# Moving 32 tokens of layer 0 from the dense expert product to the row gather

## The chip, the cores and the metric

The kernel runs on one core of a Trainium2 chip. The metric is the device time of one execution in microseconds (us). TensorE is called PE here, its weight loads PEld, VectorE is DVE, ScalarE is ACT, GpSimd is POOL, and SyncE (SP) only issues DMAs.

## What is computed

Two layers of a diffusion backbone run over 256 latent and 256 context tokens of width 1024. Each layer has a token mixer and then a PEER block, and the change is in the PEER block of layer 0, which all 512 tokens pass. PEER holds 16384 experts per layer; an expert is one row `u` and one row `v` of 1024 numbers. Each token has 8 heads, each head picks 16 experts, so a token uses 128 of them:

```
act = gelu(einsum('td,thkd->thk', xb, u_tab[eid]), approximate=False)
return einsum('thk,thkd->td', gate * act, v_tab[eid])
```

`eid` (which experts) and `gate` (a softmax over the 16 of a head) come from a routing step ahead of this.

## The kernel before

The PEER block is computed in two ways side by side.

**Dense.** Three of the four 128-token tiles of layer 0 (tiles 0, 1 and 3, so 384 tokens) are multiplied with all 16384 experts, 128 experts at a time; an "expert block" e is one of these 128 groups. `First.mm` makes the products with `u` (24 matmuls of 384 columns per block, in three split terms that keep fp32 accuracy), `First.gelu` applies the Gelu, `weigh` multiplies with the gate matrix `G` (zero for experts that a token did not pick) and splits the product `w` into `ww`, and `mm_v` multiplies with `v` (18 matmuls of 512 columns: three tiles, three split terms, two halves) into the PSUM tiles `y`. The gate matrix is built ahead of the loop, one block of 16 tokens at a time, from 0/1 rows (`find`, `weigh`, `join`, `keep`), stored in DRAM as `gd`, and read back every eighth iteration (`load_G`).

**Gathered.** Tile 2 (128 context tokens, one per partition) is computed by `gather_uv`: 128 indirect DMAs from POOL fetch one `u` row per token (`row`), DVE multiplies each with the tokens `h2` and sums it into `coef`; after a Gelu and the gate, 128 more DMAs fetch `v` rows and DVE adds them, weighted, into `f`. Six row buffers are used in turn (`NROW`).

**The order.** The main loop of `dense_experts` runs e from 0 to 127, and `in_order` holds every engine to the order in which its instructions are written. Layer 0 has worked 27 blocks of the `u` product ahead (`AHEAD0`), so iterations 0 to 100 hold a `u` product and a `v` product, and iterations 101 to 127 only the `v` product. In one iteration ACT does `act` (Gelu), `vh` (cast of a `v` block), `ww` (cast of `w`), `uh` (cast of a `u` block); DVE does `w`, `vl`, the low part of `ww`, and then the adds of the rows that the iteration before fetched; POOL does `ul` (the low part of a `u` block) and then fetches new rows. SP loads `ur` and `vr`, one block of each per iteration, in a queue of its own. How many rows have been fetched by the end of iteration e is the list `quota`: GRATE rows per iteration, and at least so many that GTAIL per iteration are left for the end. Both kinds of `row` operation stand in the helper at L859, L865 and L871; casts and low parts stand at L154 and L155.

Layer 1 works in the same way with 192 dense tokens and 64 gathered ones, which lie twice on the partitions with four heads each.

Of the kernel before, what the change touches and what calls it, by code (L numbers as in the profile page):

```python
# [19 lines left out]
D = 1024  # L20
T = 256
# [16 lines left out]
GRATE, GTAIL, HRATE = 2.4, 0.7, 1.1  # L38
# [4 lines left out]
def backbone(ctx: ExitStack, tc: tile.TileContext, x, cx, ccT, ada_w, ada_b, ada_rows, n1g, n2g, ev_in, ev_out,  # L43
# [806 lines left out]
    def gather_uv(f, eid, gate, h2, pool, quota):  # L850


        S = eid.shape[1]
        coef = pool.tile([128, S], F32, tag="coef", name="coef", bufs=1)
        r = {}

        def fetch(n):
            r[n] = pool.tile([128, D], F32, tag="row", name="row", bufs=NROW)
            nc.gpsimd.indirect_dma_start(out=r[n], out_offset=None, in_=v_tab if n >= S else u_tab,  # L859
                                         in_offset=bass.IndirectOffsetOnAxis(ap=eid[:, n % S:n % S + 1], axis=0))  # L860

        def add(n):
            t, j = r.pop(n), n - S
            if n < S:
                nc.vector.scalar_tensor_tensor(t, t, 1.0, h2, op0=OP.mult, op1=OP.mult, accum_out=coef[:, n:n + 1])  # L865
# [8 lines left out]
        for n in [*quota, 2 * S]:  # L874
# [59 lines left out]
    def dense_experts(l, slots, hi, lo, tiles, g2, upools, first, rows, half=False):  # L934
# [4 lines left out]
        ntok = nt * 128 - 64 * half  # L939
# [5 lines left out]
        with ExitStack() as st:  # L945
# [79 lines left out]
            def mm_v(*es):  # L1025
                ops = [ws.pop(e) + vs.pop(e) for e in es]
                for j in (range(nt - 1, -1, -1) if half and 127 in es else range(nt)):
                    c = slice(j * 128, (j + 1) * 128)
                    for e, (ww, vh, vl) in zip(es, ops):
                        if half and j == nt - 1:  # L1030
                            both = ww[:, full:full + 128]
                            sums = (both, vh), (both, vl)
                        else:
                            low = ww[:, 2 * ntok - full + j * 128:][:, 0:128]
                            sums = (ww[:, c], vh), (ww[:, c], vl), (low, vh)
                        for n, (x1, x2) in enumerate(sums):
                            for d in range(2):
                                nc.tensor.matmul(y[j][:, d, :], x1, x2[:, d * 512:(d + 1) * 512],  # L1038
# [3 lines left out]
            f = rp.tile([128, D], F32, tag="f", name="f")  # L1042
            if half:
                quota = [min(128, int(HRATE * (e + 1))) for e in range(128)]
# [3 lines left out]
            ys = [] if half else [(rows[0], f)]  # L1048
# [25 lines left out]
            for _ in side:  # L1074
                pass
            ab_stack.close()
# [3 lines left out]
            with in_order():  # L1080
                if half:
                    tk, yy = ys.pop()
                    t, z = (vb.tile([128, D], F32, tag="t4", name=n) for n in ("yl", "yz"))
                    nc.sync.dma_start(z[64:128], f[0:64])
# [186 lines left out]
```

## Time and profile before

| | us |
|---|---|
| median of 3 runs (lowest, highest) | 2750.55 (2741.23, 2753.81) |
| the profiled execution, whole | 2754.86 |
| its span, first to last instruction | 2752.8 |
| PE busy in the span | 2570.1 (93%) |
| DVE busy | 2055.0 (75%) |
| ACT busy | 1120.4 (41%) |
| POOL busy | 1043.0 (38%) |
| share of PE in the chain of waits that ended last | 70% |

The busy share is an average over stages that have different limits. What a change in one stage is worth is read from that stage: which wait ends last there. Four stretches of layer 0 matter here: the building of the gate matrix (from about 556 to 692 us), the main loop with `u` and `v` products (712 to 1571 us), the end of that loop with `v` products alone (1571 to 1697 us), and the routing ahead of all this.

### The profile page before, as it was taken

The page shows a single profiled execution, that of the slowest core. Times are in us where ns is not written, and L with a number is a line of the kernel's source. Part 1 is how long each engine was busy: PE and PEld are TensorE (multiplying, and loading weights), DVE is VectorE, ACT ScalarE, POOL GpSimd, SP SyncE. Part 2 cuts the span into 40 slices and gives each one's busy share as a digit, 9 for nine tenths or more (in the row PEclk, how much of TensorE's full clock was granted, in tenths as well). Part 3 has the DMA queues.
Part 4 walks back from the last instruction along what each step waited for, and adds up shares of the span by engine and source line. Part 5 has one row for each costly group of instructions (what it writes and reads, how often), then busy time and mean ns, then how long its engine had stood idle before and what let it go on. Part 6 is the DMA issues. An engine that isn't in the chain of part 4 may idle for free.

```text
span 2752.8 us, 39475 instructions
## 1 busy us (share of the span) xinstructions
PE 2570.1 (93%) x14787; PEld 2237.7 (81%) x14787; DVE 2055.0 (75%) x3753; ACT 1120.4 (41%) x1832; POOL 1043.0 (38%) x643
## 2 busy tenths in 40 slices
PE   7899996899999999999999998989859999999997
PEld 4776775899989888899898876756859899999995
DVE  3535579898677776677677776787888788888888
ACT  3234432444333333333333334234535455555543
POOL 0201042300477677667766610100520344434431
PEclk9999997899999999999999998999979999999999
DMA  8562431255888888888888875632537999999996
GB/s 285 178 207 96 138 99 33 85 207 221 293 288 287 288 287 297 286 294 298 296 308 279 289 251 165 226 129 89 179 108 257 341 347 345 348 349 332 355 326 217
DMA packets 263552, 667.80 MB, mean 243 GB/s; under 512 B 21760, under 2 KB 108544, under 8 KB 258752
## 3 DMA queue, kind: packets, MB, share of 16 engines
q1 hardware_dynamic: 204176, 458.81, 48.9%
q0 software_dynamic: 55296, 201.35, 20.2%
q10 hardware_dynamic: 3888, 5.11, 0.6%
q8 instruction: 116, 1.90, 0.3%
q14 instruction: 76, 0.62, 0.1%
HBM read 621.88 MB, written 42.47 MB: 241 GB/s over the span
## 4 chain that ended last, share of the span: by engine, by line
PE 70%; DVE 13%; issue 5%; POOL 5%; DMA 4%; ACT 1%; ACTq 0%; POOLq 0%; SPq 0%; DVEq 0%
PE y L1038 24%; PE u_ps L911 9%; PE u_ps L910 9%; PE u_ps L909 9%; PE g_ps L985 4%; PE z_ps L318 2%; PE z_ps L319 2%; PE z_ps L320 2%; POOL ul L155 2%; POOL row L859 2%; DMA w<-in_ada_w_dram 1%; PE trp L170 1%; PE q_ps L806 1%; PE q_ps L807 1%; PE q_ps L805 1%
## 5 line engine op out<-in xcount | busy, mean ns | idle before, releaser
L909 PE MATMUL u_ps<-hi,uh 128*128 128x384 f32 (+1 forms) x2048 | 635.7, 310 | 42.8 <-ACT uh L154 35.6
L1038 PE MATMUL y<-vh,ww 128*128 128x512 f32 x2304 | 661.4, 397 | 7.0 <-ACT ww L1019 6.1
L911 PE MATMUL u_ps<-hi,ul 128*128 128x384 f32 (+1 forms) x2048 | 637.5, 311 | 24.8 <-POOL ul L155 13.9
L910 PE MATMUL u_ps<-lo,uh 128*128 128x384 f32 (+1 forms) x2048 | 634.6, 310 | 0.0
L1038 PEld LDWEIGHTS y<-vh,ww 128*128 128x128 f32 x2304 | 425.0, 189 | 95.0 <-ACT ww L1019 11.4
L859 POOL DMA_INDIRECT row<-in_u_tab_dram,eid x192 | 291.4, 1518 | 424.4 <-DVE w L1015 152.0
L909 PEld LDWEIGHTS u_ps<-hi,uh 128*128 128x128 f32 x2048 | 396.0, 193 | 53.7 <-ACT uh L154 36.9
L911 PEld LDWEIGHTS u_ps<-hi,ul 128*128 128x128 f32 x2048 | 395.2, 193 | 32.5 <-POOL ul L155 20.4
L154 ACT CAST vh<-vr 128x1024 fp32r<-128x1024 f32 x256 | 267.7, 1046 | 368.4 <-PE y L1038 339.1
L1038 PE MATMUL y<-vl,ww 128*128 128x512 f32 x1280 | 402.7, 395 | 0.1
L910 PEld LDWEIGHTS u_ps<-lo,uh 128*128 128x128 f32 x2048 | 395.6, 193 | 8.7
L155 POOL TENSOR_TENSOR ul<-ur,uh 128x1024 fp32r<-128x1024 f32 x116 | 311.0, 2682 | 240.0 <-ACT uh L154 238.7
L865 DVE SCALAR_TENSOR_TENSOR row<-row,h 128x1024 f32<-128x1024 f32 x192 | 299.7, 1577 | 112.6 <-DMA row<-in_u_tab_dram,eid 112.3
L859 POOL DMA_INDIRECT row<-in_v_tab_dram,eid x192 | 288.9, 1505 | 245.0 <-DVE w L1015 142.0
L155 DVE TENSOR_TENSOR vl<-vr,vh 128x1024 fp32r<-128x1024 f32 x256 | 312.4, 1220 | 73.3 <-ACT vh L154 73.0
L871 DVE SCALAR_TENSOR_TENSOR f<-row,coef,f 128x1024 f32<-128x1024 f32 x190 | 289.9, 1526 | 100.2 <-DMA row<-in_v_tab_dram,eid 98.7
L1038 PEld LDWEIGHTS y<-vl,ww 128*128 128x128 f32 x1280 | 240.4, 188 | 59.3 <-DVE vl L155 3.9
L154 ACT CAST uh<-ur 128x1024 fp32r<-128x1024 f32 x256 | 268.3, 1048 | 20.3 <-DMA ur<-in_u_t_dram 10.9
L1019 ACT CAST ww<-w 128x384 fp32r<-128x384 f32 (+1 forms) x256 | 110.7, 432 | 330.5 <-DVE w L1015 211.6
L155 DVE TENSOR_TENSOR ul<-ur,uh 128x1024 fp32r<-128x1024 f32 x140 | 171.4, 1224 | 83.9 <-ACT uh L154 83.7
L916 ACT ACTIVATE act<-u_ps 128x384 f32<-128x384 f32 (+1 forms) x256 | 105.1, 410 | 284.8 <-PE u_ps L911 284.7
L151 POOL TENSOR_TENSOR rs<-rs,nhalf 128x4 f32<-128x4 f32 (+2 forms) x19 | 22.4, 1177 | 461.4 <-DVE rs L150 347.6
(270 smaller groups left out, 3755.9 us busy)
## 6 DMA issues: line engine op xcount, KB each, us to landing
ur<-in_u_t_dram SPq DMA_DIRECT2D x256, 512.0 KB, 5.6
vr<-in_v_tab_dram SPq DMA_DIRECT2D x256, 512.0 KB, 6.1
w<-in_ada_w_dram SPq DMA_DIRECT2D x96, 512.0 KB, 4.7
gd<-stage SPq DMA_DIRECT2D x36, 1024.0 KB, 4.8
G<-gd SPq DMA_DIRECT2D x16, 1536.0 KB, 11.9
w<-in_w_q_dram SPq DMA_DIRECT2D x64, 256.0 KB, 3.4
w<-in_od_in_dram SPq DMA_DIRECT2D x24, 512.0 KB, 5.4
G<-gd SPq DMA_DIRECT2D x16, 768.0 KB, 8.6
```

What stands on the lines that cost most here:

```text
L154: nc.scalar.copy(hi, src)
L155: (eng or nc.vector).tensor_tensor(lo, src, hi.bitcast(F32), op=OP.subtract)
L859: nc.gpsimd.indirect_dma_start(out=r[n], out_offset=None, in_=v_tab if n >= S else u_tab, in_offset=bass.IndirectOffsetOnAxis(ap=eid[:, n ...
L865: nc.vector.scalar_tensor_tensor(t, t, 1.0, h2, op0=OP.mult, op1=OP.mult, accum_out=coef[:, n:n + 1])
L871: nc.vector.scalar_tensor_tensor(f, t, coef[:, j:j + 1], f, op0=OP.mult, op1=OP.add)
L909: nc.tensor.matmul(p, uh[:, k, :], hi[:, k, 0:n], start=k == 0, stop=False)
L910: nc.tensor.matmul(p, uh[:, k, :], lo[:, k, 0:n], start=False, stop=False)
L911: nc.tensor.matmul(p, ul[:, k, :], hi[:, k, 0:n], start=False, stop=k == KD - 1)
L916: nc.scalar.activation(a, self.ps.pop(e), AF.Gelu)
L985: nc.tensor.matmul(v["p"][t // 4][:, t % 4, :], o2[:, t // 4, :, t % 4], o1[:, t // 4, :, t % 4], start=n == 0, stop=n == 1)
L1019: nc.scalar.copy(ww[:, 0:ntok], w)
L1038: nc.tensor.matmul(y[j][:, d, :], x1, x2[:, d * 512:(d + 1) * 512], start=e == 0 and n == 0, stop=e == 127 and n == len(sums) - 1)
```

## The change

32 of the 384 dense tokens of layer 0, the last 32 of tile 3, are taken out of the dense product and are gathered too. They lie four times on the 128 partitions, each quarter with two of the eight heads, so 32 more `u` rows and 32 more `v` rows are fetched per partition (`eid4`, `gate4`, `h4`). Their sums `f1` (one per quarter) are joined by a product with `quarters`, a 128 x 32 matrix of zeros and ones, straight into the last 32 partitions of `y[2]`.

- The `u` product has 352 columns in place of 384, and `act`, `w` and `ww` shrink alike. The `v` product keeps its 18 matmuls of 512 columns per block; for tile 3 they have 96 rows of output. The gate matrix has 22 blocks in place of 24.
- `gather_uv` works through two sets one after the other: 256 and then 64 rows. GRATE goes from 2.4 to 2.75 and GTAIL from 0.7 to 1.3.
- `turn_back` transposes twice as much per call and makes one more copy; three DMAs copy `h4` to the other quarters. `done` gets two DVE operations and four small DMAs per half of the heads.

```
-GRATE, GTAIL, HRATE = 2.4, 0.7, 1.1
+GRATE, GTAIL, HRATE = 2.75, 1.3, 1.1
...
-    def gather_uv(f, eid, gate, h2, pool, quota):
+    def gather_uv(sets, pool, quota):
+        todo = []
+        for f, eid, gate, h2 in sets:
+            S = eid.shape[1]
+            coef = pool.tile([128, S], F32, tag=f"coef{S}", name="coef", bufs=1)
+            todo += [(m, S, f, eid, gate, h2, coef) for m in range(2 * S)]
...
-                            low = ww[:, 2 * ntok - full + j * 128:][:, 0:128]
+                            low = ww[:, (2 * ntok - full + j * 128 if c.stop <= full else ntok):][:, 0:n_j]
...
-                quota = [min(256, int(GRATE * (e + 1)), 256 - int(GTAIL * max(0, 124 - e))) for e in range(128)]
-            side = gather_uv(f, *rows[1:], rp, quota)
+                quota = [min(total, int(GRATE * (e + 1)), total - int(GTAIL * max(0, 124 - e))) for e in range(128)]
+            side = gather_uv([(f, *r[1:]) for f, r in zip(fs, rows)], rp, quota)
...
+            if full < ntok and not half:
+                for d in range(2):
+                    nc.tensor.matmul(y[nt - 1][96:128, d, :], quarters, fs[-1][:, d * 512:(d + 1) * 512], start=True, stop=True,
+                                     tile_position=(0, 96))
...
-                    nc.scalar.copy(h2[:, k2 * 256:(k2 + 1) * 256].rearrange("p (k d) -> p k d", k=2),
-                                   transposed([h[:, k, 128:256] for k in range(2)]))
+                    p = transposed([h[:, k, c:c + 128] for c in (128, 0) for k in range(2)])
+                    c = slice(k2 * 256, k2 * 256 + 256)
+                    nc.scalar.copy(h2[:, c].rearrange("p (k d) -> p k d", k=2), p[:, 0:2])
+                    nc.scalar.copy(h4[96:128, c].rearrange("p (k d) -> p k d", k=2), p[96:128, 2:4])
+                    if k2 == 3:
+                        for g in range(3):
+                            nc.sync.dma_start(h4[32 * g:32 * g + 32], h4[96:128])
...
+                    b, eidi = slice(96, 128), wk([128, 64], "eidi", I32)
+                    nc.vector.scalar_tensor_tensor(eidf, i12[:, 0, 1, c], 128.0, i12[:, 1, 1, c], op0=OP.mult, op1=OP.add)
+                    nc.vector.tensor_copy(eidi, eidf)
+                    for g in range(2):
+                        to, h = slice(32 * (2 * r + g), 32 * (2 * r + g) + 32), slice(32 * g, 32 * g + 32)
+                        nc.sync.dma_start(eid4[to], eidi[b, h])
+                        nc.sync.dma_start(gate4[to], gate[b, 1, r * 64 + 32 * g:r * 64 + 32 * g + 32])
...
-                first = First(0, hi, lo, 384, upools)
+                first = First(0, hi, lo, 352, upools)
...
-        dense_experts(0, sl, hi, lo, (0, 1, 3), mod[5], upools, first, (2, eid, R[1][1][:, 0, :], h2))
+        dense_experts(0, sl, hi, lo, (0, 1, 3), mod[5], upools, first, 352,
+                      [(2, eid, R[1][1][:, 0, :], h2), (None, eid4, gate4, h4)])
```

The places where the change moves instructions: POOL at the start of the main loop, where `ul` is the low part of a `u` block and `row` a fetch. Before:

```order
L859 DMA row<-in_u_tab_dram,eid 128x1024 x2
L155 TENSOR_TENSOR ul<-ur,uh 128x1024
L859 DMA row<-in_u_tab_dram,eid 128x1024 x3
L155 TENSOR_TENSOR ul<-ur,uh 128x1024
L859 DMA row<-in_u_tab_dram,eid 128x1024 x2
L155 TENSOR_TENSOR ul<-ur,uh 128x1024
L859 DMA row<-in_u_tab_dram,eid 128x1024 x3
```

POOL at the same place now:

```order
L863 DMA row<-in_u_tab_dram,eid 128x1024 x3
L155 TENSOR_TENSOR ul<-ur,uh 128x1024
L863 DMA row<-in_u_tab_dram,eid 128x1024 x3
L155 TENSOR_TENSOR ul<-ur,uh 128x1024
L863 DMA row<-in_u_tab_dram,eid 128x1024 x3
L155 TENSOR_TENSOR ul<-ur,uh 128x1024
L863 DMA row<-in_u_tab_dram,eid 128x1024 x2
```

Three of four iterations fetch three rows now, where two of five did; the iteration with two rows is every fourth.

POOL around the last `ul`, after which the `v` products run alone. Before:

```order
L155 TENSOR_TENSOR ul<-ur,uh 128x1024
L859 DMA row<-in_v_tab_dram,eid 128x1024 x2
L155 TENSOR_TENSOR ul<-ur,uh 128x1024
L859 DMA row<-in_v_tab_dram,eid 128x1024 x17
L151 TENSOR_TENSOR rs<-rs,nhalf 128x2 x2
```

POOL at the same place now (`eid_2798` is `eid4`):

```order
L155 TENSOR_TENSOR ul<-ur,uh 128x1024
L863 DMA row<-in_u_tab_dram,eid_2798 128x1024 x3
L155 TENSOR_TENSOR ul<-ur,uh 128x1024
L863 DMA row<-in_u_tab_dram,eid_2798 128x1024 x13
L863 DMA row<-in_v_tab_dram,eid_2798 128x1024 x32
```

Behind the last `ul` stood 17 fetches; now 45 stand there.

SP's queue at the end of routing now, where `gate_2799` is `gate4`; before, the 11 loads of `ur` stood without a break:

```order
L901 DMA ur<-in_u_t_dram 128x1024 x10
L1164 DMA eid_2798<-eidi 32x32
L1165 DMA gate_2799<-gate_2971 32x32
L1164 DMA eid_2798<-eidi 32x32
L1165 DMA gate_2799<-gate_2971 32x32
L901 DMA ur<-in_u_t_dram 128x1024
L996 DMA gd_4830<-stage 128x2048
```

The eleventh load of `ur` now stands behind four copies that wait for the routing's last results.

## Rows read from the trace of the kernel before

**Rows 1.** Windows: us, busy us of each engine (instructions), PE clock, DMA share, GB/s

```profile
401.00:556.00 155.00, 115.97 (x567) 103.48 (x566) 146.40 (x638) 52.01 (x84) 45.24 (x36) 0.85 0.18 57
556.00:692.00 136.00, 132.19 (x979) 128.35 (x979) 116.07 (x99) 65.78 (x111) 1.24 (x2) 0.94 0.58 217
692.00:712.00 20.00, 17.88 (x92) 17.23 (x91) 6.20 (x7) 6.37 (x10) 0.87 (x1) 0.91 1.04 355
712.00:1571.00 859.00, 850.95 (x4227) 766.64 (x4226) 620.28 (x671) 297.23 (x404) 601.42 (x341) 1.00 0.84 291
1571.00:1697.00 126.00, 121.13 (x507) 96.53 (x506) 83.29 (x107) 41.66 (x57) 15.40 (x14) 0.97 0.73 243
```

**Rows 2.** Chain that ended last: start, us, what; main loop and its end

```profile
716.88 4.18 PE y L1038 x18
725.29 4.18 PE y L1038 x18
733.69 4.18 PE y L1038 x18
...
1571.50 14.89 PE y L1038 x65
```

**Rows 3.** Groups by line, 712 to 1571 us: busy, mean ns, idle before and releaser

```profile
L911 PE MATMUL u_ps<-hi,ul 128*128 128x384 f32 x809 | 275.7, 341 | 8.0 <-POOL ul L155 7.7
L155 POOL TENSOR_TENSOR ul<-ur,uh 128x1024 fp32r<-128x1024 f32 x100 | 271.9, 2719 | 218.6 <-ACT uh L154 218.2
L865 DVE SCALAR_TENSOR_TENSOR row<-row,h 128x1024 f32<-128x1024 f32 x128 | 222.1, 1756 | 112.6 <-DMA row<-in_u_tab_dram,eid 112.3
L1019 ACT CAST ww<-w 128x384 fp32r<-128x384 f32 x101 | 51.8, 513 | 170.0 <-DVE w L1015 166.2 <-PE u_ps L911 3.6
```

**Rows 4.** Timeline, one round of ACT, POOL, DVE with three rows [idle before]

```profile
848.96 0.51 ACT L1019 CAST ww<-w 128x384 fp32r<-128x384 f32 x1 [0.52 <-DVE w L1015]
...
850.51 2.41 POOL L155 TENSOR_TENSOR ul<-ur,uh 128x1024 fp32r<-128x1024 f32 x1 [0.84 <-ACT uh L154]
...
853.07 1.76 POOL L859 DMA_INDIRECT row<-in_u_tab_dram,eid  x1
855.13 1.67 POOL L859 DMA_INDIRECT row<-in_u_tab_dram,eid  x1 [0.30 <-issue]
857.11 1.80 POOL L859 DMA_INDIRECT row<-in_u_tab_dram,eid  x1 [0.30 <-issue]
...
864.94 1.23 DVE L865 SCALAR_TENSOR_TENSOR row<-row,h 128x1024 f32<-128x1024 f32 x1 [1.35 <-DMA row<-in_u_tab_dram,eid]
...
866.76 0.52 ACT L1019 CAST ww<-w 128x384 fp32r<-128x384 f32 x1 [1.51 <-DVE w L1015]
```

**Rows 5.** Timeline of ACT: casts that close the first and last three-row rounds

```profile
781.84 0.51 ACT L1019 CAST ww<-w 128x384 fp32r<-128x384 f32 x1 [1.30 <-DVE w L1015]
...
1552.45 0.51 ACT L1019 CAST ww<-w 128x384 fp32r<-128x384 f32 x1 [1.37 <-DVE w L1015]
```

**Rows 6.** The same for rounds with two rows, first and last

```profile
807.48 0.51 ACT L1019 CAST ww<-w 128x384 fp32r<-128x384 f32 x1 [1.73 <-DVE w L1015]
...
1560.77 0.51 ACT L1019 CAST ww<-w 128x384 fp32r<-128x384 f32 x1 [1.28 <-DVE w L1015]
```

**Rows 7.** Groups by line, 1571 to 1697 us

```profile
L155 DVE TENSOR_TENSOR vl<-vr,vh 128x1024 fp32r<-128x1024 f32 x26 | 31.8, 1224 | 42.1 <-ACT vh L154 42.1
L871 DVE SCALAR_TENSOR_TENSOR f<-row,coef,f 128x1024 f32<-128x1024 f32 x17 | 21.7, 1278 | 1.4 <-DMA row<-in_v_tab_dram,eid 1.4
L1022 DVE TENSOR_TENSOR ww<-w,ww 128x384 fp32r<-128x384 f32 x26 | 14.3, 551 | 0.0
```

**Rows 8.** Timeline near 1671 us: ACT's wait for a `v` block, then PE

```profile
1671.61 1.04 ACT L154 CAST vh<-vr 128x1024 fp32r<-128x1024 f32 x1 [10.23 <-DMA vr<-in_v_tab_dram]
...
1673.12 1.22 PE L1038 MATMUL y<-vh,ww 128*128 128x512 f32 x2 [4.40 <-ACT ww L1019]
...
1679.12 0.62 PE L1038 MATMUL y<-vl,ww 128*128 128x512 f32 x2
```

**Rows 9.** Chain that ended last, gate matrix: start, us, what

```profile
565.99 7.57 PE g_ps L985 x64
577.79 3.79 PE g_ps L985 x32
```

**Rows 10.** Groups by line, whole span: fp32 products of one 32-partition group

```profile
L211 PE MATMUL mod_ps<-w,silu_c 128*32 128x256 f32 x512 | 45.7, 425 | 14.7 <-DMA w<-in_ada_w_dram 8.9 <-ACT silu_c L95 5.8
```

**Rows 11.** Timeline of ACT, norm ahead of routing: one copy of `turn_back`

```profile
337.69 0.37 ACT L1126 COPY h<-trp 128x256 f32<-128x256 f32 x1 [1.28 <-PE trp L170]
```

More of the change, by code (lines that the diff above doesn't have):

```diff
@@ L873, in gather_uv @@
         done = 0
-        for n in [*quota, 2 * S]:
+        for n in [*quota, len(todo)]:
             for m in range(len(r) + done, n):
@@ L932, in step, with dense_experts @@
                 next(self.steps, None)
-    def dense_experts(l, slots, hi, lo, tiles, g2, upools, first, rows, half=False):
+    def dense_experts(l, slots, hi, lo, tiles, g2, upools, first, ntok, rows):
         nt = len(slots)
-        ntok = nt * 128 - 64 * half
+        half = ntok % 128 == 64
         ntc = ntok // 16
@@ L1037, in mm_v @@
                             for d in range(2):
-                                nc.tensor.matmul(y[j][:, d, :], x1, x2[:, d * 512:(d + 1) * 512],
+                                nc.tensor.matmul(y[j][0:n_j, d, :], x1, x2[:, d * 512:(d + 1) * 512],
                                                  start=e == 0 and n == 0, stop=e == 127 and n == len(sums) - 1)
             rp = st.enter_context(pool_(name="rp", bufs=1))
-            f = rp.tile([128, D], F32, tag="f", name="f")
+            fs = [rp.tile([128, D], F32, tag=f"f{n}", name=f"f{n}") for n in range(len(rows))]
+            total = sum(2 * r[1].shape[1] for r in rows)
             if half:
-                quota = [min(128, int(HRATE * (e + 1))) for e in range(128)]
+                quota = [min(total, int(HRATE * (e + 1))) for e in range(128)]
             else:
-                quota = [min(256, int(GRATE * (e + 1)), 256 - int(GTAIL * max(0, 124 - e))) for e in range(128)]
-            side = gather_uv(f, *rows[1:], rp, quota)
-            ys = [] if half else [(rows[0], f)]
+                quota = [min(total, int(GRATE * (e + 1)), total - int(GTAIL * max(0, 124 - e))) for e in range(128)]
+            side = gather_uv([(f, *r[1:]) for f, r in zip(fs, rows)], rp, quota)
+            ys = [(r[0], f) for f, r in zip(fs, rows) if r[0] is not None]
             for e in range(VAHEAD[l]):
@@ L1114, in expert_pools @@
             yield hi, lo, route_pools
+    quarters = const.tile([128, 32], F32, name="quarters")
+    nc.vector.tensor_add(quarters, ident[:, 0:32], ident[:, 32:64])
+    for g in (2, 3):
+        nc.vector.tensor_add(quarters, quarters, ident[:, g * 32:g * 32 + 32])
     with expert_pools(0, 512, 384, AHEAD0) as (hi, lo, route_pools):
@@ L1119, in backbone @@
         eid = gp.tile([128, 128], I32, tag="eid", name="eid")
-        h2 = gp.tile([128, D], F32, tag="h2", name="h2")
+        eid4 = gp.tile([128, 32], I32, tag="eid4", name="eid4")
+        gate4 = gp.tile([128, 32], F32, tag="gate4", name="gate4")
+        h2, h4 = (gp.tile([128, D], F32, tag=n, name=n) for n in ("h2", "h4"))
         with banks(4, 2):
@@ L1183, in backbone @@
                         slots_T(sl[i], [i12[:, 0, i, :], i12[:, 1, i, :], gate[:, i, :]])
-        dense_experts(1, sl, hi, lo, (0, 1), mod1[5], upools, first, (1, eid, hgate, h2), True)
+        dense_experts(1, sl, hi, lo, (0, 1), mod1[5], upools, first, T - 64, [(None, eid, hgate, h2)])
     fin = P["small"] = ctx.enter_context(pool_(name="fin", bufs=2))
```

23 lines of the change are left out of this document (12 added, 11 removed).

## The prediction

> **What bounds the kernel now.** I read the windows by stage first. In the main loop (712 to 1571 us) PE is busy 851 of 859 us at full clock, while DVE, ACT and POOL are busy 620, 297 and 601 us; while the gate matrix is built PE is busy 132 of 136 us; at the end, with `v` products alone, 121 of 126 us; in the routing it is DVE, 146 of 155 us [rows 1]. So from 556 us on the short answer is PE. The chain of waits says the same: the `v` products start every 8.40 to 8.41 us, and one takes 4.18 us, so a `u` product takes the other 4.22 us [rows 2].
>
> But 100 periods, from the first start to the one at 1571.50, take 854.6 us, or 8.55 each: 0.14 us more than PE's own 8.41 [rows 2]. So something reaches PE now and then, and the groups by line say what. PE waited for POOL's `ul`, though only 7.7 us in all. POOL waited 218 us for the cast `uh`, ACT waited 166 us for DVE's `w`, and DVE waited 112 us for rows that POOL had fetched [rows 3]. These waits form a ring, and one round of it is in the timeline: cast `ww` at 848.96, then `uh` on ACT, `ul` on POOL at 850.51, three fetches at 853.07, 855.13 and 857.11, the third row landed and added at 864.94 (7.8 us after its issue), `w`, and `ww` again at 866.76 [rows 4]. That is 17.80 us, and it spans two iterations, for which PE needs 16.82 us. The ring is slower than PE in this round; PE notices little, because `ww` and `ul` are ready some us ahead of their use.
>
> I measured all 98 rounds in this stretch, each from a `ww` to the second `ww` behind it, by the number of rows fetched in between. The 39 with three rows average 17.73 us, the 59 with two 16.71 us; 34 and 43 of them end in a wait for DVE, and of those the closing casts of the first and the last are shown [rows 5, 6]. The mix, 0.4 x 17.73 + 0.6 x 16.71 = 17.12, or 8.56 a period, is the 8.55 of the chain. **PE and the ring are level now**: that is the point on which the forecast rests.
>
> **The main loop.** The change shortens each `u` matmul by 32 of 384 columns: 4.22 x 32/384 = 0.35 us per block, so that PE's own period becomes 8.06 us. It also puts three rows where two stood: the pattern 2, 2, 3, 2, 3 becomes 2, 3, 3, 3. The third row costs the ring one more POOL issue (2.06 us from start to start in [rows 4]) and one more landing. With the measured rounds, 0.75 x 17.73 + 0.25 x 16.71 = 17.48, or 8.74 a period. `w`, `ww` and its low part shrink by a twelfth (some 0.05 us each of 0.5), so I take 8.72. Over 100 periods: 872 - 854.6 = **+17 us**. The bounds: if PE kept the pace with today's loss of 0.14, 8.20 a period, -35 us; if the strand of rounds that never has a two-row iteration set the pace (the two-row iteration is every fourth, so it always falls into the same one of the two interleaved rings), 17.73 / 2 = 8.87, +32 us. The value taken lies near the upper one because the two kinds of round are measured, and a PE pace of 16.12 us for two periods is below the mean of both.
>
> On the 0.35 us: the trace gives 4.22 / 24 = 0.176 us from one `u` matmul to the next. The Trainium skill (TensorE: Matmul & The Clock Gate, section "Wait — 56ns, not 53.3ns?") has N / 2.4 GHz and a fixed 2.5 ns, which would be 0.163 us; by it the fixed part doesn't shrink, and the saving would be 0.32 us per block. PE's period would then be 8.09, and the lower bound 3 us less of a gain.
>
> **The end, `v` products alone.** 28 blocks of 4.18 us are 117 us; the stretch takes 126. The difference is a wait of 4.40 us for `ww` that waited for a `v` block, and what followed: the matmuls from 1673.12 to 1679.12 ran at about half rate (1.22 us for a pair against 0.62), some 2.7 us [rows 8]. The order of POOL's queue shows 45 fetches behind the last `ul` now, where 17 stood. These 28 rows have to be moved, and added at 1.28 us each [rows 7]. If spread evenly they would fit: DMA moves 243 GB/s there, and in the stretches at 0.84 and 1.04 of its share 291 and 355 GB/s, so about 345 is full; 126 us leave room for 12.9 MB, or 24 rows of 0.524 MB, and DVE has 43 us idle for 36 us of adds [rows 1, 7]. They aren't spread: up to about iteration 108 the rate stays at 2.75 rows. An iteration then moves 3.75 x 0.524 MB = 1.97 MB, 5.7 us at 345 GB/s, and DVE needs 0.5 + 1.22 + 0.5 + 2.75 x 1.28 = 5.7 us too; PE needs 4.18. Eight iterations cost 12 us. The two loads of G that fall into this stretch, 1.4 MB each, meet fuller queues than now; I add one more wait such as the one shown, with its slow matmuls, 7 us. **+19 us**; at least 0 (spread and hidden), at most 28 x 1.52 = +43 us (every row on the path).
>
> **The gate matrix.** Two blocks of 24 go, each 3.79 us of PE (7.57 for two) [rows 9], and 12 `u` products in this stretch save 0.35 us each: 7.6 + 4.2 = **-12 us**. PE is the limit there; DVE, next at 116 us, loses work with the same two blocks. The other 15 products ahead of the loop lie beside the routing, where DVE is the limit, or beside the loads at 692 to 712 us with DMA at 1.04 [rows 1], and save nothing.
>
> **What is added ahead of the loop and behind it.** Four more ACT copies of at most 0.37 us [rows 11] stand in the norm; four more DVE operations of 64 columns in the routing cost less than the 0.55 us of one of 384 columns each [rows 7]. The DMAs of `h4` stand on SP ahead of later `w_q` loads, those of `eid4` and `gate4` ahead of the eleventh `ur` load, which has three buffers and is needed only blocks later: nothing, if that cover holds, and a few us of the routing if not. The join is two fp32 products on 32 output partitions with 512 columns; the nearest row has 0.425 us for 256 columns [rows 10], so at most 1.7 us, and DVE still has a tile to gate then. Together **+3 us**, from 0 to +6.
>
> **Sum.** +17 + 19 - 12 + 3 = +27 us on the profiled execution of 2754.9 us: 2782. That execution lies 4.3 us above the median of the three runs, so the forecast of the median is **2778 us**.
>
> **The rivals.**
> - *PE keeps the pace in the main loop (faster).* For it: in calm stretches `ww` isn't late at all, and PE's waits sum to only 8 us [rows 3]. If POOL and DVE hinder each other only where both read at once, an iteration needs `ul` 2.41 [rows 4], and DVE's 0.5 + 1.22 + 0.5 and 1.22 per row: 8.29 with three rows, 7.07 with two, mean 7.98, under 8.06. This is the lock of the Trainium skill (SBUF — State Buffer, section "Who interferes with whom"): VectorE operations with two SBUF inputs and GpSimd operations that read SBUF exclude each other. The trace agrees that they do: the add takes 1756 ns on average beside `ul`, 1278 without [rows 3, 7]. Against it: the latency of the rows isn't in that sum, and the rounds show it. Price: -35 + 12 - 12 + 3 = -32, so 2719 us.
> - *The ring stays at today's 8.55 (no change).* Rounds with two rows were partly held at PE's pace, and could be shorter without it; a load of G that disturbs the ring is a little smaller. Main loop 0, the end +9, then -12 and +3: 2751 us.
> - *The end runs out of DMA (slower still).* Six fetched rows, a `v` block and G queue together, `v` blocks come late again and again, and PE, idle often, falls to the lower clock as at 1673 us. Together with the slower strand in the main loop: +32 + 43 - 12 + 3 = +66, so 2817 us. It decides from the point where two blocks of `v` ahead no longer cover the queue.
> - That the change doesn't do what it says is excluded by the order: 22 gate blocks, 352 columns, 45 fetches at the end.
>
> **How the numbers follow.** The forecast has 0.45, with a range of its own of 2762 to 2795 (8.65 to 8.80 a period, the end +10 to +27); PE's pace 0.22, no change 0.20, the end 0.13. A measurement of this kernel can tell about 0.5% from no change, here 13.8 us. From 2719 to 2817 leaves about half of the fastest and half of the slowest case out, less than 2 in 10. Faster: the first rival and a little of the second, 0.23. Within: most of the second and the lower end of the forecast, 0.20. Slower: 0.57.
>
> **What would show it.** In the profile after: starts of `v` products about 8.7 us apart in the main loop with PE waiting for `ul` and `ww` for many us (the rival: 8.1 and hardly any); rounds of two iterations still near 17.7 us; PE busy well under 99% there; the stretch with `v` products alone about 145 us, its first eight iterations at 5 to 6 us; the gate matrix in about 124 us. The forecast is wrong if rounds with three rows get shorter once PE doesn't hold them, or if fetches wait less for DVE than they do now.

## The result, and the profile after

The changed kernel takes 2814.5 us (median of 6 runs, 2811.0 to 2829.5); the kernel before, run beside it, 2746.7 us (2741.2 to 2753.8). The ratio is 1.0258, 95% interval 1.0231 to 1.0286: slower, by some 68 us where 27 were forecast.

The profiled execution of the changed kernel took 2828.1 us whole, 73.2 more than the profiled one of before (2754.9). By the starts of the stages, those 73 us lie here:

| stage (us) | before | after | difference | forecast |
|---|---|---|---|---|
| start of the gate matrix | 556.9 | 565.4 | +8.4 | +3 (with the join) |
| gate matrix and loads, to the first `v` product | 160.0 | 139.7 | -20.3 | -12 |
| main loop, 100 periods | 854.6 | 903.0 | +48.4 | +17 |
| end, `v` products alone | 125.5 | 161.7 | +36.2 | +19 |

The rows behind the table, start of the gate matrix before, as the chain of waits has it:

```profile
556.91 3.83 PE g_ps L985 x31
```

and the four starts of the changed kernel, the first and the last from the chain of waits, the others from the timeline of PE:

```profile
565.35 3.84 PE g_ps L990 x31
...
705.01 0.62 PE L1044 MATMUL y<-vh,ww 128*128 128x512 f32 x2
...
1608.06 0.63 PE L1044 MATMUL y<-vh,ww 128*128 128x512 f32 x2
...
1767.97 1.85 PE y L1085 x4
```

The last one is the join, which the forecast has in its +3 and the table in the 161.7 us of the end. The profiled executions are not quite typical: that of the changed kernel lies 13.5 us above its median, that of before 8.1. The same main loop took 899.4 us in another execution (the run with `GTAIL` 1.8), and that of before 847.7 and 843.5 us in the two runs with an altered front; so the differences by stage hold to some 10 us.

The windows of the changed kernel by the same stages (us; then busy us of PE, PEld, DVE, ACT, POOL with their instructions; granted PE clock, DMA share, GB/s), which answer to [rows 1]:

```profile
401.00:565.00 164.00, 117.57 (x588) 103.28 (x587) 155.03 (x675) 54.68 (x88) 46.38 (x39) 0.86 0.18 58
565.00:685.00 120.00, 118.68 (x916) 115.94 (x916) 106.09 (x91) 60.11 (x103) 0.00 (x0) 0.97 0.61 227
685.00:705.00 20.00, 18.88 (x117) 18.30 (x117) 6.49 (x9) 7.51 (x13) 2.11 (x2) 1.00 1.02 330
705.00:1608.00 903.00, 840.87 (x4202) 731.90 (x4201) 664.85 (x823) 287.89 (x401) 658.04 (x376) 0.97 0.85 296
1608.00:1770.00 162.00, 129.38 (x510) 93.07 (x508) 118.84 (x180) 41.00 (x58) 57.88 (x43) 0.92 0.81 282
```

In the main loop PE is busy 841 of 903 us, where it was busy 851 of 859; at the end 129 of 162, where it was 121 of 126. No other engine is near its limit in either. So PE waits, and the groups by line of the main loop (705 to 1608 us; busy us, mean ns of one | idle us before it and what ended it) say for whom:

```profile
L155 POOL TENSOR_TENSOR ul<-ur,uh 128x1024 fp32r<-128x1024 f32 x100 | 281.9, 2819 | 187.4 <-ACT uh L154 186.5
L916 PE MATMUL u_ps<-hi,ul 128*128 128x352 f32 x801 | 273.4, 341 | 54.4 <-POOL ul L155 54.4
L914 PE MATMUL u_ps<-hi,uh 128*128 128x352 f32 x800 | 270.2, 338 | 7.7 <-ACT uh L154 7.7
L870 DVE SCALAR_TENSOR_TENSOR row<-row,h 128x1024 f32<-128x1024 f32 x147 | 246.4, 1692 | 122.9 <-DMA row<-in_u_tab_dram,eid 122.4
L876 DVE SCALAR_TENSOR_TENSOR f<-row,coef,f 128x1024 f32<-128x1024 f32 x127 | 212.1, 1670 | 114.0 <-DMA row<-in_v_tab_dram,eid 107.6 <-issue 4.9
L1024 ACT CAST ww<-w 128x352 fp32r<-128x352 f32 x100 | 48.7, 487 | 319.6 <-DVE w L1020 312.3 <-PE y L1044 7.2
```

This is the ring of [rows 3] in the same order: PE waits 54.4 us for POOL's `ul` (7.7 before), ACT 312 us for DVE's `w` (166), DVE 230 us for `u` and `v` rows (210). Only POOL waits less for the cast `uh` (187 us, 218 before), being busy itself for 658 us instead of 601.

The loss isn't spread evenly. Near a load of G it looks like this, in the timeline of ACT, DVE, POOL and PE (start, duration, [idle before, and what ended it]):

```profile
988.12 1.05 ACT L154 CAST vh<-vr 128x1024 fp32r<-128x1024 f32 x1 [2.20 <-PE y L1044]
...
988.64 1.23 DVE L870 SCALAR_TENSOR_TENSOR row<-row,h 128x1024 f32<-128x1024 f32 x1 [2.98 <-DMA row<-in_u_tab_dram,eid]
...
991.40 1.23 DVE L870 SCALAR_TENSOR_TENSOR row<-row,h 128x1024 f32<-128x1024 f32 x1 [1.54 <-DMA row<-in_u_tab_dram,eid]
...
994.55 1.23 DVE L870 SCALAR_TENSOR_TENSOR row<-row,h 128x1024 f32<-128x1024 f32 x1 [1.91 <-DMA row<-in_u_tab_dram,eid]
...
996.33 0.49 ACT L1024 CAST ww<-w 128x352 fp32r<-128x352 f32 x1 [7.16 <-PE y L1044]
...
997.84 3.35 POOL L155 TENSOR_TENSOR ul<-ur,uh 128x1024 fp32r<-128x1024 f32 x1 [7.08 <-ACT uh L154]
...
1001.25 0.66 PE L916 MATMUL u_ps<-hi,ul 128*128 128x352 f32 x1 [2.85 <-POOL ul L155]
```

Three rows land late one after the other; `w` comes at 995.70, `ww` at 996.33, 8.2 us behind the cast `vh` of its iteration, and POOL and PE follow. (The wait of 7.16 us is put down to PE, whose `y` products had long been done; ACT waited for `w`.) The windows of the same stretch, with the columns as above, show the cause at one end and the price at the other:

```profile
988.00:992.00 4.00, 4.00 (x25) 3.89 (x24) 1.83 (x3) 1.05 (x1) 2.29 (x3) 1.00 1.02 416
992.00:996.00 4.00, 4.00 (x20) 3.21 (x19) 2.09 (x5) 0.00 (x0) 0.00 (x0) 1.00 1.01 409
996.00:1000.00 4.00, 1.30 (x6) 0.49 (x4) 3.50 (x7) 2.73 (x4) 2.16 (x1) 0.89 0.53 172
1000.00:1004.00 4.00, 2.75 (x9) 2.75 (x10) 4.00 (x6) 1.17 (x2) 3.54 (x3) 0.50 0.48 145
```

While G and the rows come in, the DMA moves 409 to 416 GB/s at a share of 1; then PE, after a stretch in which it was busy 1.30 of 4 us, runs its next products at a granted clock of 0.50, the lower of its two levels (1.2 GHz).

At the end, the first load of G stands in the queue ahead of the `v` blocks (the timeline of SP's queue, then ACT, POOL and PE):

```profile
1621.18 0.43 SPq L1015 DMA_DIRECT2D G<-gd  x1
1624.52 43.61 SPq L957 DMA_DIRECT2D vr<-in_v_tab_dram  x7
...
1644.41 1.04 ACT L154 CAST vh<-vr 128x1024 fp32r<-128x1024 f32 x1 [13.18 <-DMA vr<-in_v_tab_dram]
...
1648.38 1.86 POOL L863 DMA_INDIRECT row<-in_v_tab_dram,eid  x1 [11.74 <-DVE f L874]
...
1645.90 1.22 PE L1044 MATMUL y<-vh,ww 128*128 128x512 f32 x2 [10.02 <-ACT ww L1024]
```

A `v` block that was asked for at 1624.5 us is there at 1644.4; PE stands 10 us and then runs a pair in 1.22 us, as in [rows 8]. Two more such waits follow in the timeline of PE, one behind the second load of G (issued at 1672.76 us) and one where the kernel before had its only one, of 4.40 us:

```profile
1695.38 1.22 PE L1044 MATMUL y<-vh,ww 128*128 128x512 f32 x2 [8.46 <-ACT ww L1024]
...
1744.21 1.22 PE L1044 MATMUL y<-vh,ww 128*128 128x512 f32 x2 [9.38 <-ACT ww L1024]
```

Over the whole end PE waits 32 us for `ww`, against 4.8 before.

### The profile page after: what moved, and what is told of

It is laid out like the page before. It is cut to its first block, busy times and chain, and to the rows that moved or that the text cites. A ratio compares the mean times of both kernels' runs of the same rounds, so it can differ in the third digit from the quotient of the medians.

```text
span 2826.2 us, 39766 instructions
## 1 busy us (share of the span) xinstructions
PE 2557.2 (90%) x14735; PEld 2187.6 (77%) x14735; DVE 2128.6 (75%) x3977; ACT 1108.2 (39%) x1829; POOL 1139.7 (40%) x707
## 4 chain that ended last, share of the span: by engine, by line
PE 51%; DVE 15%; issue 13%; POOL 11%; DMA 8%; ACT 2%; SPq 0%; POOLq 0%; ACTq 0%; DVEq 0%
PE y L1044 15%; POOL row L863 7%; PE u_ps L916 6%; PE u_ps L915 5%; PE u_ps L914 5%; POOL ul L155 4%; PE g_ps L990 3%; PE z_ps L318 2%; PE z_ps L319 2%; PE z_ps L320 2%; DMA vr<-in_v_tab_dram 2%; DMA row<-in_v_tab_dram,eid 2%; DVE f L876 1%; PE trp L170 1%; PE mod_ps L211 1%
## 5 line engine op out<-in xcount | busy, mean ns | idle before, releaser
L916 PE MATMUL u_ps<-hi,ul 128*128 128x352 f32 (+1 forms) x2048 | 634.0, 310 | 73.9 <-POOL ul L155 60.6
L1044 PE MATMUL y<-vh,ww 128*128 128x512 f32 (+1 forms) x2304 | 665.5, 398 | 34.6 <-ACT ww L1024 33.8
L914 PE MATMUL u_ps<-hi,uh 128*128 128x352 f32 (+1 forms) x2048 | 630.3, 308 | 51.7 <-ACT uh L154 44.2
L915 PE MATMUL u_ps<-lo,uh 128*128 128x352 f32 (+1 forms) x2048 | 627.5, 306 | 0.0
L1044 PEld LDWEIGHTS y<-vh,ww 128*128 128x128 f32 (+1 forms) x2304 | 410.2, 184 | 137.7 <-ACT ww L1024 42.7
L863 POOL DMA_INDIRECT row<-in_u_tab_dram,eid x224 | 335.4, 1497 | 429.0 <-DVE w L1020 152.2
L863 POOL DMA_INDIRECT row<-in_v_tab_dram,eid x224 | 333.8, 1490 | 252.3 <-DVE w L1020 141.2
L876 DVE SCALAR_TENSOR_TENSOR f<-row,coef,f 128x1024 f32<-128x1024 f32 x221 | 332.5, 1504 | 114.6 <-DMA row<-in_v_tab_dram,eid 107.6
L1024 ACT CAST ww<-w 128x352 fp32r<-128x352 f32 (+1 forms) x256 | 107.4, 420 | 511.9 <-DVE w L1020 390.2
L921 ACT ACTIVATE act<-u_ps 128x352 f32<-128x352 f32 (+1 forms) x256 | 101.4, 396 | 239.8 <-PE u_ps L916 238.1
```

The costliest lines, as they stand in the source:

```text
L876: nc.vector.scalar_tensor_tensor(f, t, coef[:, j:j + 1], f, op0=OP.mult, op1=OP.add)
L914: nc.tensor.matmul(p, uh[:, k, :], hi[:, k, 0:n], start=k == 0, stop=False)
L915: nc.tensor.matmul(p, uh[:, k, :], lo[:, k, 0:n], start=False, stop=False)
L916: nc.tensor.matmul(p, ul[:, k, :], hi[:, k, 0:n], start=False, stop=k == KD - 1)
L921: nc.scalar.activation(a, self.ps.pop(e), AF.Gelu)
L1024: nc.scalar.copy(ww[:, 0:ntok], w)
```

## The experiments

All times are medians beside the kernel before on the same chip (2743 to 2749 us); stage times are of one profiled execution each.

**The ring, cut at ACT.** One step moved in the changed kernel:

```
+                    if not half:
+                        first.split(e + R + 1, nc.gpsimd)
                     weigh(e + 1)
-                    first.split(e + R + 1, nc.vector if half else nc.gpsimd)
```

(Layer 1 keeps the old order.)

> The changed kernel with one step moved: in layer 0 the casts uh and ul of the next u block are written ahead of w, so on ACT uh no longer stands behind ww, and POOL's ul and the row fetches behind it no longer wait for DVE's row adds. Nothing is left out. Changed kernel: 2814.5 us, main loop 9.03 us per period, of which PE needs 8.0. Ring theory (the fetches wait for a cast that waits for the row adds, so a late row makes the next fetches late): opened here, so the main loop falls to 8.0 to 8.4 per period, 60 to 100 us less, 2715 to 2755 us. Rival, the queues (a G load of 1.41 MB fills the DMA queues at about 410 GB/s, and rows are late whoever issues them when): the two long iterations at every G load stay, at most a third of the loss of 100 us goes, 2780 or more. Rival, DVE and POOL shut each other out: the sum of their work is unchanged, 2810 to 2815.

Measured: 2728.4 us, ratio to before 0.9923 (0.9901 to 0.9945): 86 us less than the changed kernel, and less than the kernel before. The groups by line of its main loop (698 to 1505 us), same columns as above:

```profile
L155 POOL TENSOR_TENSOR ul<-ur,uh 128x1024 fp32r<-128x1024 f32 x100 | 278.8, 2788 | 134.2 <-ACT uh L154 134.1
L916 PE MATMUL u_ps<-hi,ul 128*128 128x352 f32 x800 | 259.2, 324 | 0.0
L1020 DVE TENSOR_TENSOR w<-G,act 128x352 f32<-128x352 f32 x100 | 202.0, 2020 | 0.0
L870 DVE SCALAR_TENSOR_TENSOR row<-row,h 128x1024 f32<-128x1024 f32 x148 | 189.1, 1324 | 1.6 <-DMA row<-in_u_tab_dram,eid 1.6
```

PE waits for nothing, and DVE hardly ever for a row: 807.7 us for 100 periods, 8.08 each. Yet the rows come no sooner. The DMA issues between 760 and 1400 us (count, median us from issue to landing), first of the kernel before:

```profile
row<-in_u_tab_dram,eid POOLq DMA_INDIRECT x114, 6.6
```

and then of this one:

```profile
row<-in_u_tab_dram,eid POOLq DMA_INDIRECT x104, 8.1
```

They take 1.5 us longer and nobody waits, because a late row no longer makes the next fetch late. The two rivals that need no ring fall with this.

**The ring, cut at POOL.** In the changed kernel `next(side)` is written ahead of `first.split` (in layer 0), and nothing else is moved.

> The changed kernel with the ring cut at another link: the row fetches (and the adds that stand ahead of them) are written ahead of uh and ul of the same iteration, so on POOL a fetch no longer stands behind this iteration's ul, while uh still stands behind ww on ACT. Nothing is left out. Ring theory: a fetch now hangs on the ul of the iteration before, so the same chain of work is spread over three iterations (24 us of PE) and not over two (16), and the main loop falls from 9.03 to 8.1 to 8.4 us per period, as with uh moved: 2725 to 2755 us. If moving uh helped for another reason (ACT free earlier, the u block in time whatever the rows do), the fetches' place changes nothing: 8.9 to 9.1 per period, about 2810.

Measured: 2726.3 us (two runs; 0.9934, 0.9916 to 0.9953), main loop 802.1 us. Its groups by line, 705 to 1507 us:

```profile
L870 DVE SCALAR_TENSOR_TENSOR row<-row,h 128x1024 f32<-128x1024 f32 x149 | 299.2, 2053 | 0.0
L155 POOL TENSOR_TENSOR ul<-ur,uh 128x1024 fp32r<-128x1024 f32 x100 | 289.6, 2896 | 41.4 <-ACT uh L154 40.1
L916 PE MATMUL u_ps<-hi,ul 128*128 128x352 f32 x800 | 257.3, 322 | 1.9 <-POOL ul L155 1.9
```

A different link, the same 8.0 us per period. That the loss is the ring's is shown twice.

**The shorter `u` product alone.** The 32 tokens are taken out of the dense product and not gathered; the kernel leaves them out of its result. The rows go by the old rates.

```
-GRATE, GTAIL, HRATE = 2.75, 1.3, 1.1
+GRATE, GTAIL, HRATE = 2.4, 0.7, 1.1
...
-                      [(2, eid, R[1][1][:, 0, :], h2), (None, eid4, gate4, h4)])
+                      [(2, eid, R[1][1][:, 0, :], h2)])
```

> The changed kernel without its second set of rows: the 32 tokens are taken out of the dense product, but not gathered (they are left out of the result), and GRATE and GTAIL are 2.4 and 0.7 as before, so 256 rows in the pattern 2, 2, 3, 2, 3 with 17 at the end. It shows what the shorter u product is worth with the rows as they were. Ring theory: the rounds stay as in the kernel before (8.55 per period, a little less since G loads are a twelfth smaller), so the main loop gains 0 to 15 us, and with the gate matrix (20 us) the whole is 2715 to 2735. Rival, PE kept the pace and the rings only followed: 8.2 per period, 35 us less in the main loop, 2690 to 2705.

Measured: 2728.7 us (0.9923, 0.9888 to 0.9957). The main loop takes 838.1 us, 8.38 per period, the end 126.4. Its window:

```profile
708.00:1546.00 838.00, 814.37 (x4201) 712.33 (x4200) 608.26 (x766) 288.17 (x400) 597.51 (x341) 0.99 0.86 295
```

Of the 35 us that PE could gain in the loop 16 are there by the profiled execution of before, 5 to 10 by the two executions with an altered front; the rest PE spends waiting (814 us busy of 838). The 64 rows of the second set then cost 65 us in the main loop (903.0 - 838.1) and 35 at the end (161.7 - 126.4).

**The row pattern alone.** In the kernel before, `GRATE` 2.75 in place of 2.4.

> The kernel before (384 columns, one set of 256 rows) with GRATE 2.75 in place of 2.4: three rows in three of four iterations until 227 rows are fetched (about 83 iterations), then 0.7 per iteration. Nothing is left out. It shows the row pattern without the shorter u product. By the prediction's step (three-row rounds 17.73 us, two-row rounds 16.71, measured at the old pattern) the first 80 periods take 8.74 each; if the pattern itself makes the rounds longer (three-row rounds next to each other, and the G load always at the same place of the pattern), 8.9 to 9.05 each, as in the changed kernel. The last 17 periods, with few rows, take 8.41 in both cases, so the whole comes out 5 to 30 us above the kernel before.

Measured: 2789.5 us (one run). The windows of the main loop, first the 83 periods with three rows in three of four iterations, then the 17 with few:

```profile
716.00:1462.00 746.00, 714.41 (x3487) 638.57 (x3486) 550.19 (x605) 244.31 (x333) 542.15 (x310) 0.99 0.85 297
1462.00:1605.00 143.00, 143.00 (x716) 129.57 (x715) 83.39 (x65) 48.47 (x67) 64.98 (x33) 1.00 0.60 189
```

From the `v` product at 716.37 to the one at 1462.61 a period takes 8.99 us, and from there to 1605.54 8.41. The changed kernel, with `u` products 32 columns shorter, takes 9.03. So at this pattern the ring alone sets the pace, and shorter products of PE win nothing. Rounds, measured from `ww` to the second `ww` behind it: three-row rounds 18.22 us on average, two-row rounds 17.54; in the changed kernel 18.24 (74) and 17.61 (24). In the kernel before they were 17.73 and 16.71.

**G in pieces.** In the changed kernel each load of G is cut into six, one per iteration:

```
+                    c = slice(0, ntc) if part is None else slice(part * 4, min(part * 4 + 4, ntc))
+                    if c.start < ntc:
+                        nc.sync.dma_start(G[b][:, c], gd[c, :, b * 8:b * 8 + 8, :].rearrange("c p i t -> p c i t"))
...
-                    if e % 8 == 0:
-                        load_G(e // 8 + 1)
+                    if not half:
+                        load_G(e // 8 + 1, e % 8)
```

> The changed kernel with the G load of every eighth iteration (1.41 MB at once) cut into six pieces of at most 4 of the 22 blocks, one piece per iteration. Nothing is left out. Changed kernel: 2814.5 us; of the 8.4 us that 8 iterations lose against PE's 64, some 5.7 us are lost in the two or three iterations at the G load (12 loads in the main loop, 2 at the end). Queues theory: without the lump these 5.7 us go at each load, and the end loses its wait of 10 us: 70 to 80 us less, about 2740. Ring theory alone: a round with three rows keeps its 17.7 us also in calm stretches, so a period stays at 8.7 or more: 10 to 35 us less, 2780 to 2805.

Measured: 2801.5 us (1.0190, 1.0145 to 1.0235), 13 us less than the changed kernel. By the profiled executions, which differ by 24, it is more: main loop 891.3 us (12 less), end 144.6 (17 less). Two-row rounds fall from 17.61 to 16.96 us; three-row rounds stay (18.16). The load of G is the occasion of the longest waits, but a small part of the loss: without the lump the ring takes 8.91.

**The end, spread.** `GTAIL` 1.8 in place of 1.3 in the changed kernel.

> The changed kernel with GTAIL 1.8 in place of 1.3: the 44 rows that are left for the end are fetched at 1.8 per iteration throughout instead of 2.75 in the first eight iterations and 1.3 afterwards; the main loop is the same. Nothing is left out. The end took 161.7 us, of which 117 are PE's. If the end is long because the first eight iterations ask for more than the DMA queues move (1.97 MB per iteration beside a G load): the waits of 10 and 4 us there go, the end takes 130 to 145 us, 15 to 30 us less, 2785 to 2800. If it is the number of rows (45 instead of 17) that counts, wherever they stand, it stays at 155 to 165, and the whole at 2808 to 2820.

Measured: 2815.8 us (1.0250, 1.0205 to 1.0296), as the changed kernel. In the profiled execution the end takes 149.8 us, 12 less, but the time doesn't show it; a gain below some 10 us can't be told by these intervals, so this run is inconclusive.

**Rows out of the end.** The opened ring (as in the first run), with `GRATE` 3.02 and `GTAIL` 0.7.

> The changed kernel with the ring opened (uh and ul ahead of w; 2728.4 us, main loop 8.08 per period, end 158.9) and GRATE 3.02, GTAIL 0.7: three rows in every iteration of the main loop, 17 left for the end as in the kernel before. Nothing is left out. If the rows decide what the end costs, it falls from 158.9 to about 126 us; if the G loads and the v blocks alone fill the queues there, it stays above 145. If POOL has room for three fetches per iteration once the ring is open (it was busy 613 of 807 us), the main loop stays at 8.1 and the whole comes to 2693 to 2700; if not, the main loop pays back 15 to 30 us, 2710 to 2730.

Measured: 2697.5 us (0.9825, 0.9803 to 0.9847). Its windows, main loop and end:

```profile
701.00:1509.00 808.00, 808.00 (x4203) 712.57 (x4202) 777.35 (x871) 293.93 (x406) 677.07 (x406) 1.00 0.96 350
1509.00:1634.00 125.00, 121.22 (x509) 91.12 (x507) 83.68 (x133) 39.61 (x55) 14.13 (x12) 0.99 0.74 239
```

The end falls from 158.9 to 125.3 us, and the main loop takes the 28 rows for nothing. So the rows that are left for the end are what it costs, and in the main loop, once the ring is open, there was room for them.

**Three edits, four, and the fair comparison.** The opened ring with G in pieces and `GTAIL` 1.8:

> The changed kernel with three edits together: uh and ul ahead of w, the G load in six pieces, GTAIL 1.8. Nothing is left out. The first gives the main loop of 8.08 per period. If the end (158.9 us) is long because a G load and the rows meet in the same iterations, the pieces and the even rate bring it to 125 to 135: 2695 to 2705. If the 45 rows and the v blocks fill the queues in any order (45.7 MB in this stretch and the loads behind it, at about 400 GB/s 114 us of PE's 117), it stays at 140 to 150: 2710 to 2720.

Measured: 2702.3 us (0.9864, 0.9825 to 0.9903), main loop 799.3, end 137.3. With G in pieces and an even rate, 21.6 of the 33 us that the rows cost at the end are gone, and 12 are left.

The opened ring with `GRATE` 3.02, `GTAIL` 0.7 and G in pieces:

> The changed kernel with the ring opened (uh and ul ahead of w), three rows per iteration (GRATE 3.02, GTAIL 0.7, 17 rows left for the end) and the G load in six pieces. Nothing is left out. Without the pieces 2697.5 us, main loop 8.08 per period, end 125.3. If the G loads as lumps still cost the end its 8 us above PE's 117 and the u products some us, the main loop comes to 799 to 803 and the end to 118 to 121: 2682 to 2690. If they cost nothing there any more, 2695 to 2700.

Measured: 2691.4 us, 0.9799 (0.9781 to 0.9817), the fastest of all and 2% below the kernel before; main loop 807.7, end 124.9. That lies between the two cases of the expectation. Against 2697.5 without the pieces the stages show no difference, and the intervals overlap: the pieces win little or nothing here.

The kernel before with its ring opened in the same way:

> The kernel before (384 dense tokens) with the one step moved that opened the ring in the changed kernel: uh and ul of the next u block are written ahead of w. Nothing is left out. Kernel before: about 2749 us, main loop 8.55 us per period. If PE and the ring were level, as the prediction says, opening the ring can win no more than the 0.14 us per period that PE lost: main loop 840 to 846 us, whole 2733 to 2742. If PE's 8.41 was itself stretched by the ring (PE slow because its operands come just in time), more than that: below 2725.

Measured: 2742.4 us (0.9983, 0.9969 to 0.9996), main loop 840.7, or 8.41 per period:

```profile
718.00:1559.00 841.00, 841.00 (x4204) 762.13 (x4203) 548.49 (x672) 289.40 (x401) 543.26 (x343) 1.00 0.85 298
```

Opening the ring alone is worth next to nothing there. On the opened ring the change, with its rows moved out of the end, is worth 45 us (2742.4 to 2697.5). The profiled executions differ by 43: 33 in the main loop and 20 in the gate matrix, less 3 in front, 2 at the end and 5 behind it.

**The front.** The kernel before with one of the two additions ahead of the loop, unused: first those of `turn_back`, then those of `done`.

> The kernel before with the added work of turn_back alone: twice the transposes, one more ACT copy per call, the three copies of h4 between partitions; h4 is not used. Nothing is left out. In three executions of kernels with the old front the gate matrix began at 548.8 to 551.0 us, in seven with the new front at 551.2 to 558.5 (mean 556.1). By the prediction's step this part adds 0 to 2 us: start at 549 to 553. If the DMAs of h4 push the w_q loads back, 554 or later.

> The kernel before with the added work of done alone: four DVE operations and eight small DMAs for eid4 and gate4, which are not used. Nothing is left out. By the prediction's step DVE, the limit there, gains at most some 1 to 2 us of work: the gate matrix begins at 550 to 553 us. If the small DMAs, which stand on SP ahead of a ur load, hold back the u products that run beside the routing, 554 or later.

Measured, by the first product of the gate matrix (549.9 us in the profiled execution of before, 558.3 in that of the changed kernel; the table above counts from the chain's first piece of it, 7 us later): it begins at 551.7 and 551.6 us, 1.8 and 1.7 above the mean of the three executions with the old front (548.8 to 551.0); the times of the single runs (2747.9 and 2747.1) lie within those of the kernel before. In nine executions with the whole new front it begins at 551.2 to 558.5 us, mean 556.1, so 6.2 later. The two parts together would make 3.5 of it, but each is one execution, and the nine spread over 7 us: this is a hint, and where the rest comes from is not shown.

## Why the prediction was right in the way and wrong in the size

**What bounds the kernel** was right: PE and a ring through `ww`, `uh`, `ul`, fetch, landing, add and `w` stand level in the kernel before. Both cuts show the ring, and the kernel before with its ring opened shows how level: 8.41 against 8.55. Even that 0.14 was large: in the two executions with an altered front the same loop has 8.48 and 8.43 a period.

**The main loop: +17 forecast, +48 measured. The step that failed is "with the measured rounds, 0.75 x 17.73 + 0.25 x 16.71 = 17.48".** PE's own pace was a little better than forecast and had no part in it: a `u` block takes 3.82 us, 0.159 from one matmul to the next, and so saves 0.40, more than the 0.35 of a plain proportion. By the rule of the Trainium skill that was weighed there (TensorE: Matmul & The Clock Gate, section "Wait — 56ns, not 53.3ns?") it would have been 0.32; this trace bears out neither. The rounds' weights were right, their lengths were not: 18.24 and 17.61 give 18.09, or 9.04 a period, as measured. The lengths had been read where every three-row round lay between two-row rounds, and were carried to a pattern where each has a three-row round beside it. The two interleaved rings share POOL and DVE, and a round depends on its neighbour. I sorted them by the rounds that start one iteration before and one behind. In the changed kernel three-row rounds take 17.1 us behind a two-row round, 18.6 between three-row rounds and 19.1 ahead of a two-row round; with G in pieces 17.5, 18.8 and 18.2. The middle ones show how: `ul` starts 3.0 us behind `ww` there, and 1.5 in the other two, since POOL is still fetching for the round before. One such round in the timelines of ACT and POOL:

```profile
858.85 0.49 ACT L1024 CAST ww<-w 128x352 fp32r<-128x352 f32 x1 [3.77 <-DVE w L1020]
859.25 1.04 ACT L154 CAST uh<-ur 128x1024 fp32r<-128x1024 f32 x1
...
861.00 0.94 POOL L863 DMA_INDIRECT row<-in_u_tab_dram,eid  x1 [0.31 <-issue]
861.95 2.39 POOL L155 TENSOR_TENSOR ul<-ur,uh 128x1024 fp32r<-128x1024 f32 x1
```

Over all three-row rounds the stretch from `ww` to the start of the last fetch grew from 7.75 to 8.81 us; the stretch behind the last fetch shrank by 0.55. In the two-row rounds the stretch behind the last fetch grew from 10.0 to 11.6 us, and falls to 10.4 with G in pieces: every eighth iteration's load of G now always meets the same place of a pattern that repeats every four. So 8 to 12 of the 31 missing us go with G's lump (891.3 us with pieces, against 899.4 and 903.0 in the two executions with the lump), and the other 19 to 23 stand in rounds made longer by their neighbours. Why the tail of a two-row round is still 0.4 longer without the lump isn't settled. The landing time itself isn't it: a median of 6.6 us before, 6.7 at the new pattern with 384 columns.

The lower bound, 8.20, was passed only once the ring was cut; the upper one, 8.87, was no bound, since it used the same 17.73.

**The end: +19 forecast, +36 measured.** The cause was right, 45 fetches instead of 17 and waits for `v` blocks; the term that was mis-sized is "one more wait such as the one shown, 7 us". There were two more on PE, 10.0 and 8.5 us, one behind each load of G, and the one shown grew from 4.4 to 9.4. The first eight iterations took 49.7 us, 6.2 each instead of 5.7, with the wait of 10.0 in them. The forecast counted the DMA's capacity over whole iterations; the queue, with G's 1.41 MB ahead of the `v` blocks, held one of them for 20 us. That the rows "aren't spread" was only a part of it. By the forecast's own sum 28 rows don't quite fit when spread, since there was room for 24; with the ring open, pieces of G and an even rate still leave 12 us of the 33, and with 17 rows left for the end nothing is left of them.

**The gate matrix: -12 forecast, -20 measured.** From 556.9 to 692 it took 135 us, now 119.6: -15.5. Two blocks are 7.6 us of it; ten `u` products stand there, not twelve, but each saves 0.41 us instead of 0.35, which is 4.1; three waits of PE of 1.0 us each in between became one, which is 1.9. The ten `u` products together went from 44.8 to 39.2 us; the 1.5 us above those 4.1 lie in three that ran in part at a lower granted clock before (0.50 from 560 to 562 us, 0.87 from 630 to 634 and from 671 to 675). The last 0.4 are not accounted for. The remaining 4.9 us lie behind it, in the loads before the first `v` product (24.9 to 20.0 us), which the forecast had held to save nothing: five shorter `u` products are 2 us of it, and the load of G was issued 5.7 us behind the last gate product instead of 7.5.

**Ahead of the loop: +3 forecast, +8.4 in the profiled execution, +6.2 in the mean of nine.** The forecast's upper end was 6. The join took 1.85 us, against at most 1.7. One place shows in the traces: a `vl` of the routing takes 3.05 to 3.11 us beside POOL's `ul` in all ten executions with the additions of `done`, and 1.21 in the four others, which is 1.9 us of DVE, the limit there. An operation that is shifted can fall beside another engine's; its own cost is not its price.

**The rivals.** "The end runs out of DMA" is the one that came true at the end, and its 2817 us are within 3 of the measured time, though its main loop was worked out too short (8.87) and its end too long (+43). That these errors and those of the gate matrix and the front cancel to 3 us is luck. It had 0.13; its condition, two blocks of `v` ahead that no longer cover the queue, is what the timeline at 1621 to 1644 us shows. "PE keeps the pace" was wrong for this order of instructions, but its sum of work was right: with the ring cut, DVE and POOL, who do hold each other up (a row add of 2053 ns, a `w` of 2020), still keep under PE's 8.0. (The 1756 ns that it took for an add beside `ul` is a mean over both kinds: from 720 to 1500 us of the kernel before the 61 adds of `u` rows that overlap a `ul` take 2307 ns, the 65 others 1222.) "The ring stays at 8.55" falls.

What was named to show it did show: `v` products 9.0 us apart with PE waiting, PE busy 93% in the loop, and the gate matrix in 120 us. The rounds "still near 17.7" did not, and the `v` products alone took 161.7 us instead of some 145.

## What to carry to other kernels

A ring of waits through four engines that is level with the busiest engine has no room for what is added to its links; look for the one cast or fetch that stands behind a wait it doesn't need, and move that first. Here a change that lost 68 us wins 45, against the kernel before with the same step moved, once `uh` may go ahead of `ww` and the rows are moved out of the end into the room that this makes. A round's length belongs to the pattern in which it was measured: when the neighbours change, measure it there (a run with the new pattern and nothing else would have given 9.0).

## What the runs showed of the hardware that was not expected

Where DVE and POOL hold each other up, the wait is booked as busy time of whatever DVE operation stands beside `ul`. The same `w` of 352 columns took 518 ns on average in the changed kernel and 2020 with `uh` moved (shown above), while the row adds fell from 1692 to 1324. In the groups by line of the changed kernel:

```profile
L1020 DVE TENSOR_TENSOR w<-G,act 128x352 f32<-128x352 f32 x100 | 51.8, 518 | 0.0
```

With `uh` moved, from 720 to 1500 us, the 77 `w` that overlap a `ul` take 2440 ns and the 21 others 519. The Trainium skill (SBUF — State Buffer, section "Who interferes with whom") has such a lock between the two. The trace agrees by these two means. Busy shares of DVE can therefore rise (777 of 808 us in the run with the rows early) without DVE being the bound.

Short stalls of PE cost more than their length: after the stretch of 1.30 busy us in 4 shown above, `u` matmuls started 0.29 us apart instead of 0.16 from 1001.7 to 1005.8 us. The granted clock was 0.50 in the window from 1000 us, 0.76 from 1004 and 1.00 from 1008.

The DMA moved up to 416 GB/s in the stretches with G, against the 345 to 355 that the forecast had taken as full.

With `uh` moved a `u` block took 3.81 and 3.99 us by turns, with no wait recorded, in the run with that edit alone and in both with `GRATE` 3.02; it took 3.81 all through with `GTAIL` 1.8 and G in pieces, and nearly so with the fetches moved instead. That is some 8 us of the main loop (807.7 against 799.3), and its cause stays open.
